# Three tiles of the MLP's up projection, instead of two, taken token group by token group

## The chip, the cores and the metric

The kernel runs on one core of one Trainium2 chip. The metric is the time of one execution in microseconds (us), the median of several runs.

## The reference, cut to what matters

Two layers of a backbone over 512 latent tokens and 256 context tokens, width 1024, in float32. Each layer ends with an MLP whose hidden width is 4096; the second layer computes it for the latent tokens alone.

```python
def sq_relu_mlp(h, w1, w2):
    return jnp.square(jax.nn.relu(h @ w1)) @ w2

        x = x + g1 * ox
        x = x + g2 * sq_relu_mlp(modulate(rmsnorm(x, norm_mlp[l]), sh2, sc2), w_ff1[l], w_ff2[l])
        if not last:
            h = h + cg1 * oc
            h = h + cg2 * sq_relu_mlp(modulate(rmsnorm(h, norm_mlp[l]), csh2, csc2), w_ff1[l], w_ff2[l])
```

## The kernel before, in words

All activations stand transposed: 128 channels on the partitions, tokens along the free axis. Latent and context tokens lie side by side, 768 columns in layer 0 and 512 in layer 1. A float32 product is made of three float32r matmuls (`mm3`, all issued by line 220): operands are split into a high part (a rounded copy, ScalarE, line 228) and a low part (the difference, VectorE, line 237), and hi x hi, hi x lo and lo x hi are summed in PSUM.

The program is a list of tasks. `emit` (line 279) walks through it; ahead of each task it starts the loads of coming weights and splits up to four pieces of 128 x 512 ahead (`AP_`), of which at most six live at once (`N_W`, tiles `wt`). The Tile scheduler then puts each engine's instructions into a fixed order; each engine runs its own in that order.

**Ahead of the MLP** the output projection's last tiles (`res`) are computed token group by token group. The groups are columns 0 to 255, 256 to 511 and, in layer 0 alone, 512 to 767. When a group's `x` is complete, its RMS norm follows: the sum of squares by a matmul (`ssum`), then per channel tile `hn` (VectorE, line 572), the high part of `h` (ScalarE, line 575) and its low part (VectorE, line 576). The norm of the last group is the list `first` in `layer_ff`.

**The MLP** (`layer_ff`, line 1347) goes by chunks of the hidden width: 4 tiles of 128 hidden channels in a chunk in layer 0, 8 in layer 1. An up tile (`up`) is 8 x 3 matmuls per part: two halves of 384 columns in layer 0, one of 512 columns in layer 1 (PSUM tiles `f`, called f1 in the order). Only the first tiles of the first chunk go another way (`up_two`, line 1455): for one token group at a time, over all k, for all of these tiles, with matmuls of 256 columns. The norm of the last group (`first`) stands in the list between group 0 and the others.

The evacuation (`evac`) takes relu (ScalarE, line 1437) and the square (line 1439) into `b`; `sums` makes the seven operands of a Strassen product from a pair of tiles and their two token halves: differences `T` (VectorE, lines 1391 and 1392), and for each operand the high part (line 228) and the low part (line 237) in `act`.

The down projection (`block`, `product`; PSUM tiles f2) multiplies them in the order A11, S1, A12, S4, S3, S2, A22 with quarters of the weights or sums of quarters (`sum`, VectorE, line 264); each product is evacuated by a gate into `x` (VectorE, line 1481), a copy to `V` (ScalarE, line 1489) or an addition to it. In layer 0 a block has two products of 6 matmuls per weight piece, in layer 1 one of 12.

Beside all this VectorE makes the adaLN modulation of later stages as dot products (`rows`, `dot`, line 492), whose weights come through three buffers.

Of the kernel before, what the change touches and what calls it, by code (L numbers as in the profile page):

```python
# [144 lines left out]
def merge(*streams):  # L145

    total = [max(sum(t.cost for t in s), 1e-9) for s in streams]
    done = [0.0] * len(streams)
    at = [0] * len(streams)
    out = []  # L150
    while True:
        live = [i for i in range(len(streams)) if at[i] < len(streams[i])]
        if not live:
            return out
        i = min(live, key=lambda j: (done[j] + 0.5 * streams[j][at[j]].cost) / total[j])
        t = streams[i][at[i]]
        at[i] += 1
        done[i] += t.cost
        out.append(t)


class Net:
# [1184 lines left out]
    def layer_ff(self, l, whole, groups, first):  # L1347
# [83 lines left out]
        def evac(c, m, half, parts):  # L1431

            if half in (0, None):
                st["b", m % 2] = self.tmp("b")
            b = st["b", m % 2]
            for ps, at, n in parts:
                nc.scalar.activation(b[:, at:at + n], ps, AF.Relu)  # L1437
            o, n = (0, w) if half is None else (half * hw, hw)
            nc.scalar.activation(b[:, o:o + n], b[:, o:o + n], AF.Square)
            if c == n_chunk - 1:  # L1440
                split_plain(c, m, half)
                return
            for i in (0, 1) if half is None else (half,):
                sums(c, m, i)

        def up(c, m, u):
            for half in (None,) if last else range(2):
                o, n = (half * hw, hw) if half is not None else (0, w)
                ps = self.B([P, 512], "f1")
                for k in range(NK):  # L1450
                    s = slice(k * P, (k + 1) * P)
                    self.mm3(ps[:, :n], u[:, 0, s], u[:, 1, s], H(k)[:, 0, o:o + n], H(k)[:, 1, o:o + n], k == 0, k == NK - 1)
                evac(c, m, half, [(ps[:, :n], o, n)])

        def up_two(us, i):

            if i == 0:
                st["pair"] = [self.R("f1") for _ in us]
            ps = st["pair"]
            o, n, _ = groups[i]  # L1460
            for k in range(NK):
                s = slice(k * P, (k + 1) * P)
                for j, u in enumerate(us):
                    self.mm3(ps[j][:, o:o + n], u[:, 0, s], u[:, 1, s],
                             H(k)[:, 0, o:o + n], H(k)[:, 1, o:o + n], k == 0, k == NK - 1)
            if i < len(groups) - 1:
                return
            for j in range(2):
                for half in range(2):
                    o, e = half * hw, half * hw + hw  # L1470
                    cut = [(max(o, x), min(e, x + 512)) for x in range(0, w, 512)]
                    evac(0, j, half, [(ps[j][:, x:y], x, y - x) for x, y in cut if x < y])
# [37 lines left out]
        def block(c, blk, u):  # L1510
            cost = 3 * CP * hw / 2.2
            return [Task(cost, lambda i=i, n=n: product(c, u, i, MP * blk + i, n), (u.pieces[n],))
                    for n in (A11, S1, A12, S4, S3, S2, A22) for i in range(MP)]

        def finish(j):

            U, v5, v7 = (st[n][j] for n in "U57")
            add(v7, v7, U)
            gate(2 * j + 1, 0, v7, True)
            add(U, U, v5)  # L1520
            add(v7, v7, v5)
            gate(2 * j, 1, U)
            gate(2 * j + 1, 1, v7, True)
# [24 lines left out]
        for c in range(n_chunk):  # L1548
            us = [Unit(a["w_ff1"][l, 2 * CP * c + m], 1024) for m in range(2 * CP)]
            m0, ups = 0, []  # L1550
            cost = self.lin_cost(NK, [(0, hw)] * 2)
            if c == 0:
                m0 = 2
                pair = [Task(2 * cost / len(groups), lambda us=us, i=i: up_two(us[:2], i), tuple(us[:2]))
                        for i in range(len(groups))]
                out += [Task(0, begin), pair[0]] + first + pair[1:]
            for m in range(m0, 2 * CP):
                ups.append(Task(cost, lambda c=c, m=m, u=us[m]: up(c, m, u), (us[m],)))
            if c == 0:
                ups.append(Task(0, negate))  # L1560
            if c == n_chunk - 1:
                ups = merge(ups, [Task(1, lambda j=j: finish(j)) for j in range(4)])
            blocks = [Unit(a["w_ff2"][l, c * n_blk + blk], 2048, "st") for blk in range(n_blk)]
            downs = []
            if c < n_chunk - 1:
                for blk in range(n_blk):
                    downs += block(c, blk, blocks[blk])
            share = -(-len(spread) // max(n_chunk - 1 - c, 1))
            extra, spread = spread[:share], spread[share:]
            if c == 0:  # L1570
                out += merge(ups, self.extra.pop(("ff1", l), []))
                out += merge(downs, extra)
            else:
                out += merge(ups, extra) + downs if l == 0 else merge(ups + downs, extra)
# [199 lines left out]
```

## Time and profile before

| | |
|---|---|
| median of 3 runs | 1567.8 us (1564.02 to 1570.93) |
| the profiled execution: its time, its span | 1565.01 us, 1562.9 us |
| TensorE (PE) busy | 1506.0 us, 96% |
| VectorE (DVE) busy | 1190.1 us, 76% |
| ScalarE (ACT) busy | 797.0 us, 51% |
| GpSimd (POOL) busy | 37.9 us, 2% |
| DMA | 191.98 MB moved, mean 123 GB/s |

Busy shares are averages over the whole span. Stretches of it have other limits, so the order of time of each engine is read at the places where the change acts: in layer 0 from about 395 to 475 us, in layer 1 from about 1195 to 1290 us. A line of the order of time gives start, length, engine, source line, operation, what is written from what, and how many instructions are merged; in square brackets stands how long the engine was idle before and what ended that.

### The profile page before, as it was taken

Reading aid. Unit: us, or ns where it says so; the run is one execution under the profiler, and the core shown is the slowest. Engines: PE = TensorE matmul, PEld = TensorE weight load, DVE = VectorE, ACT = ScalarE, POOL = GpSimd, SP = SyncE. Lnnn points to the kernel's source line nnn. Section 1 sums busy time; section 2 is a strip of 40 time slices with the busy share of each in tenths; the row PEclk is TensorE's granted clock in tenths of the full one; section 3 lists DMA queues with packets and bytes.
Section 4 is the critical chain, followed back from the end, with each engine's and each line's share of the span. In section 5 each row is a group of like instructions: output and inputs, shape, how many; then the busy total and the mean of one; then the engine's idle time right before and its main releaser. Section 6 shows DMA issues by size and latency. Waiting matters only on the chain.

```text
span 1562.9 us, 24541 instructions
## 1 busy us (share of the span) xinstructions
PE 1506.0 (96%) x9120; PEld 1329.2 (85%) x9120; DVE 1190.1 (76%) x2633; ACT 797.0 (51%) x1635; POOL 37.9 (2%) x78
## 2 busy tenths in 40 slices
PE   5999999999999999999999999989999999999997
PEld 2798667888899999999999998757888898989886
DVE  6668765887997887878869696997647895968844
ACT  4425467653654344344443463566655655455443
POOL 0110001000000000000000002001000000000000
PEclk9999999999999999999999999999999999999999
DMA  9463454555132413322223227547433443242321
GB/s 359 136 186 101 133 137 95 173 180 187 48 108 89 129 49 106 100 68 90 75 75 114 81 96 230 177 125 189 152 97 113 155 120 97 82 127 72 126 81 54
DMA packets 68903, 191.98 MB, mean 123 GB/s; under 512 B 8752, under 2 KB 11312, under 8 KB 68784
## 3 DMA queue, kind: packets, MB, share of 16 engines
q1 hardware_dynamic: 65440, 180.18, 36.6%
q0 software_dynamic: 2816, 9.70, 2.7%
q8 instruction: 72, 1.18, 0.3%
q10 hardware_dynamic: 528, 0.52, 0.1%
q14 instruction: 47, 0.39, 0.1%
HBM read 159.97 MB, written 10.49 MB: 109 GB/s over the span
## 4 chain that ended last, share of the span: by engine, by line
PE 83%; DVE 9%; ACT 3%; DMA 3%; issue 1%; SPq 0%; DVEq 0%; ACTq 0%
PE f L220 49%; PE A L220 9%; PE sc L220 4%; PE oe L220 3%; PE res L220 3%; PE pv L220 3%; PE rv L220 2%; PE pT L1052 2%; DMA rows<-w_adaT 2%; PE ada L220 1%; DVE wt L237 1%; DVE hn L572 1%; DVE h L576 1%; DVE rows L492 1%; PE ro L220 1%
## 5 line engine op out<-in xcount | busy, mean ns | idle before, releaser
L220 PE MATMUL f<-h,wt 128*128 128x384 f32 (+2 forms) x2400 | 454.3, 351 | 4.2 <-ACT h L575 3.5
L220 PEld LDWEIGHTS f<-h,wt 128*128 128x128 f32 x2400 | 416.8, 189 | 38.6 <-ACT h L575 4.5
L220 PE MATMUL f<-act,wt 128*128 128x256 f32 (+2 forms) x2664 | 410.0, 315 | 1.0 <-ACT wt L228 0.7
L220 PEld LDWEIGHTS f<-act,wt 128*128 128x128 f32 x2664 | 394.0, 188 | 15.7 <-ACT wt L228 3.5
L237 DVE TENSOR_TENSOR wt<-raw,wt 128x512 fp32r<-128x512 f32 x326 | 222.6, 687 | 101.2 <-ACT wt L228 99.9
L228 ACT ACTIVATE wt<-raw 128x512 fp32r<-128x512 f32 x326 | 198.7, 626 | 166.9 <-PE f L220 67.4
L220 PE MATMUL A<-h,wt 128*128 128x512 f32 (+1 forms) x912 | 172.9, 347 | 3.4 <-ACT h L575 2.4
L220 PEld LDWEIGHTS A<-h,wt 128*128 128x128 f32 x912 | 142.8, 190 | 29.5 <-ACT h L575 3.1
L228 ACT ACTIVATE wt<-sum 128x512 fp32r<-128x512 f32 x104 | 62.7, 629 | 126.8 <-DVE sum L264 103.4
L1437 ACT ACTIVATE b<-f 128x384 f32<-128x384 f32 (+3 forms) x100 | 50.6, 510 | 139.4 <-PE f L220 139.2
L492 DVE SCALAR_TENSOR_TENSOR rows<-rows,sbc 128x512 f32<-128x512 f32 x136 | 92.0, 685 | 8.1 <-DMA rows<-w_adaT 7.5
L220 PE MATMUL sc<-k,q 96*128 96x512 f32 (+1 forms) x384 | 87.2, 356 | 8.4 <-ACT p L1034 7.4
L220 PEld LDWEIGHTS sc<-k,q 96*128 96x128 f32 x384 | 64.4, 193 | 26.3 <-ACT p L1034 10.3
L237 DVE TENSOR_TENSOR wt<-sum,wt 128x512 fp32r<-128x512 f32 x104 | 70.3, 686 | 8.3 <-ACT wt L228 7.0
L1033 DVE TENSOR_REDUCE st<-sc 128x1 f32<-128x768 f32 x64 | 60.8, 952 | 13.7 <-PE sc L220 13.1
L1481 DVE SCALAR_TENSOR_TENSOR x<-f,mod,x 128x256 f32<-128x256 f32 (+2 forms) x148 | 69.6, 502 | 0.5 <-ACT V L1489 0.4
L1053 ACT ACTIVATE pT<-pT 128x384 f32<-128x384 f32 x128 | 56.8, 492 | 23.5 <-PE pT L1052 22.8
L228 ACT ACTIVATE act<-T 128x384 fp32r<-128x384 f32 (+1 forms) x104 | 47.3, 473 | 40.5 <-DVE T L1392 28.0
L1391 DVE TENSOR_TENSOR V<-V,f 128x384 f32<-128x384 f32 (+1 forms) x136 | 66.2, 513 | 0.1
L1034 ACT ACTIVATE p<-sc,st 128x768 f32<-128x768 f32 x64 | 57.9, 905 | 14.5 <-DVE st L1033 13.4
L220 PE MATMUL oe<-mix,wt 128*128 128x512 f32 (+1 forms) x288 | 60.8, 363 | 0.0
L237 DVE TENSOR_TENSOR act<-b,act 128x384 fp32r<-128x384 f32 (+2 forms) x94 | 47.4, 514 | 16.9 <-ACT act L228 16.9
(244 smaller groups left out, 1837.9 us busy)
## 6 DMA issues: line engine op xcount, KB each, us to landing
raw<-w_ff SPq DMA_DIRECT2D x128, 512.0 KB, 3.7
rows<-w_adaT SPq DMA_DIRECT2D x136, 256.0 KB, 3.2
raw<-w_in SPq DMA_DIRECT2D x22, 512.0 KB, 4.2
raw<-w_ada SPq DMA_DIRECT2D x16, 512.0 KB, 10.1
raw<-w_out SPq DMA_DIRECT2D x16, 512.0 KB, 4.2
rows<-w_ada SPq DMA_DIRECT2D x24, 256.0 KB, 3.1
x<-xd SPq DMA_DIRECT2D x6, 768.0 KB, 8.1
x<-xT SPq DMA_DIRECT2D x4, 768.0 KB, 6.5
```

Source lines behind the costliest of these rows:

```text
L220: return self.nc.tensor.matmul(out, l, r, start=start, stop=stop)
L228: self.nc.scalar.activation(out, src, AF.Copy, **k)
L237: return self.nc.vector.tensor_tensor(out, src, hi.bitcast(F32), op=ALU.subtract)
L492: nc.vector.scalar_tensor_tensor(out, w, 1.0, self.sbc[:, v, half], op0=ALU.mult, op1=ALU.mult, accum_out=acc[:, v, i, j:j + 1])
L572: nc.vector.scalar_tensor_tensor(t[:, :n], self.X(k)[:, o:o + n], G, self.ss[:, 1, o:o + n], op0=ALU.mult, op1=ALU.mult)
L1033: nc.vector.tensor_reduce(st[:, 0:1], ps, axis=AX, op=ALU.max, negate=True)
L1034: nc.scalar.activation(p, ps, AF.Exp, bias=st[:, 0:1], accum_out=st[:, 1:2])
L1052: nc.tensor.transpose(ps[:, kt, :], p[:, (k0 + kt) * P:(k0 + kt + 1) * P], self.ident)
L1053: nc.scalar.activation(s["pT", h, qt // 2][:, k0:k0 + 3, c], ps, AF.Copy)
L1391: add = lambda x, y, z, op=ALU.add: nc.vector.tensor_tensor(x, y, z, op=op)
L1437: nc.scalar.activation(b[:, at:at + n], ps, AF.Relu)
L1481: self.mark = nc.vector.scalar_tensor_tensor(x, ps[:, at - o:at - o + n], g[:, cond:cond + 1], x, op0=ALU.mult, op1=ALU.add)
```

## The change

The first three tiles of the first chunk are taken group by group, not two. `up` then begins with the fourth tile.

```diff
-        def up_two(us, i):
+        def up_three(us, i):
...
             if i < len(groups) - 1:
                 return
-            for j in range(2):
+            for j in range(3):
                 for half in range(2):
...
             if c == 0:
-                m0 = 2
-                pair = [Task(2 * cost / len(groups), lambda us=us, i=i: up_two(us[:2], i), tuple(us[:2]))
+                m0 = 3
+                pair = [Task(3 * cost / len(groups), lambda us=us, i=i: up_three(us[:3], i), tuple(us[:3]))
                         for i in range(len(groups))]
                 out += [Task(0, begin), pair[0]] + first + pair[1:]
```

What moves is seen in the engines' orders.

TensorE, layer 0, where group 2 begins. f1_838 and f1_839 are tiles 1 and 2 on groups 0 and 1, f1_854 and f1_855 the same tiles on group 2, and f1_873 is tile 3, columns 0 to 383. Before:

```order
L220 MATMUL f1_838_4299<-h7_790_4071,wt_770_3972 128x256 x3
L220 MATMUL f1_839_4303<-h7_790_4071,wt_820_4226 128x256 x3
L220 MATMUL f1_854_4446<-h0_783_4064,wt_769_3969 128x256
L220 MATMUL f1_855_4450<-h0_783_4064,wt_819_4223 128x256
L220 MATMUL f1_873_4555<-h0_783_4064,wt_836_4293 128x384 x3
L220 MATMUL f1_854_4446<-h0_783_4064,wt_769_3969 128x256 x2
L220 MATMUL f1_855_4450<-h0_783_4064,wt_819_4223 128x256 x2
L220 MATMUL f1_854_4446<-h1_784_4065,wt_769_3969 128x256 x3
L220 MATMUL f1_855_4450<-h1_784_4065,wt_819_4223 128x256 x3
```

Now, ahead of the same place (f1_840 is tile 3 on groups 0 and 1; group 2's f1_855 to f1_857 come after it):

```order
L220 MATMUL f1_840_4307<-h0_783_4064,wt_836_4293 128x256
L220 MATMUL f1_840_4307<-h1_784_4065,wt_836_4293 128x256 x3
L220 MATMUL f1_840_4307<-h2_785_4066,wt_836_4293 128x256 x3
L220 MATMUL f1_840_4307<-h3_786_4067,wt_836_4293 128x256 x3
L220 MATMUL f1_840_4307<-h4_787_4068,wt_837_4296 128x256 x3
L220 MATMUL f1_840_4307<-h5_788_4069,wt_837_4296 128x256 x3
L220 MATMUL f1_840_4307<-h6_789_4070,wt_837_4296 128x256 x3
L220 MATMUL f1_840_4307<-h7_790_4071,wt_837_4296 128x256 x3
L220 MATMUL f1_840_4307<-h0_783_4064,wt_836_4293 128x256 x3
L220 MATMUL f1_840_4307<-h1_784_4065,wt_836_4293 128x256 x3
```

All 48 matmuls of tile 3 on groups 0 and 1 now stand before group 2; 3 of 384 columns stood in its first rows before.

VectorE, layer 0, from the last low part of `h` to the first differences `T` of the evacuation. Before:

```order
L237 TENSOR_TENSOR wt_864_4532<-raw_771_3975,wt_864_4532 128x512
L576 SCALAR_TENSOR_TENSOR h6_789_4070<-hn_852_4390,mod0_108,h6_789_4070 128x256
L576 SCALAR_TENSOR_TENSOR h7_790_4071<-hn_853_4394,mod0_108,h7_790_4071 128x256
L237 TENSOR_TENSOR wt_865_4535<-raw_771_3975,wt_865_4535 128x512
L237 TENSOR_TENSOR act_857_4499<-b_856_4496,act_857_4499 128x384
L237 TENSOR_TENSOR wt_870_4547<-raw_821_4229,wt_870_4547 128x512
L1391 TENSOR_TENSOR T_858_4505<-b_856_4496 128x384
```

Now:

```order
L576 SCALAR_TENSOR_TENSOR h6_789_4070<-hn_853_4415,mod0_108,h6_789_4070 128x256
L576 SCALAR_TENSOR_TENSOR h7_790_4071<-hn_854_4419,mod0_108,h7_790_4071 128x256
L237 TENSOR_TENSOR act_859_4573<-b_858_4570,act_859_4573 128x384
L237 TENSOR_TENSOR wt_869_4619<-raw_771_3975,wt_869_4619 128x512
L237 TENSOR_TENSOR wt_870_4622<-raw_771_3975,wt_870_4622 128x512
L237 TENSOR_TENSOR wt_873_4629<-raw_821_4229,wt_873_4629 128x512
L1391 TENSOR_TENSOR T_860_4579<-b_858_4570 128x384
```

The same three weight pieces and one `act` stand before `T`; `T` reads `b` of tile 1, which needs group 2 of that tile.

TensorE, layer 1, where group 1 begins. Before, it follows group 0 of tiles 1 and 2 at once (f1_2258, f1_2259; f1_2289 is tile 3, 512 columns):

```order
L220 MATMUL f1_2259_12548<-h4_2230_12430,wt_2239_12467 128x256
L220 MATMUL f1_2259_12548<-h5_2231_12431,wt_2239_12467 128x256
L220 MATMUL f1_2259_12548<-h4_2230_12430,wt_2239_12467 128x256
L220 MATMUL f1_2258_12544<-h0_2226_12426,wt_2213_12334 128x256
L220 MATMUL f1_2259_12548<-h0_2226_12426,wt_2238_12464 128x256
L220 MATMUL f1_2289_12744<-h0_2226_12426,wt_2255_12536 128x512
```

Now, a little ahead of the same place (f1_2260 is tile 3):

```order
L220 MATMUL f1_2259_12573<-h4_2230_12455,wt_2239_12492 128x256
L220 MATMUL f1_2260_12577<-h0_2226_12451,wt_2255_12561 128x256 x2
L220 MATMUL f1_2260_12577<-h1_2227_12452,wt_2255_12561 128x256
L220 MATMUL f1_2260_12577<-h0_2226_12451,wt_2255_12561 128x256
L220 MATMUL f1_2260_12577<-h1_2227_12452,wt_2255_12561 128x256 x3
L220 MATMUL f1_2260_12577<-h2_2228_12453,wt_2255_12561 128x256 x3
L220 MATMUL f1_2260_12577<-h2_2228_12453,wt_2256_12564 128x256
L220 MATMUL f1_2260_12577<-h3_2229_12454,wt_2256_12564 128x256
```

The 24 matmuls of tile 3 on group 0 stand before group 1, 22 of them at this place. VectorE's order in layer 1 has, ahead of the first `T`, one weight piece (wt_2287) that stood behind it before.

## Rows read from the trace of the kernel before

**Rows 1.** The page, part 1: busy us, share of span, instructions.
```profile
PE 1506.0 (96%) x9120; PEld 1329.2 (85%) x9120; DVE 1190.1 (76%) x2633; ACT 797.0 (51%) x1635; POOL 37.9 (2%) x78
```
**Rows 2.** TensorE in order of time, layer 0, MLP start: start, us, work, [idle before].
```profile
409.70 3.71 PE L220 MATMUL f<-h,wt 128*128 128x256 f32 x28
414.93 10.36 PE L220 MATMUL f<-h,wt 128*128 128x256 f32 x72 [1.52 <-ACT h L575]
```
**Rows 3.** TensorE in order of time, layer 1, MLP start.
```profile
1203.13 2.09 PE L220 MATMUL f<-h,wt 128*128 128x256 f32 x12
1207.16 9.12 PE L220 MATMUL f<-h,wt 128*128 128x256 f32 x54 [1.95 <-ACT h L575]
```
**Rows 4.** TensorE's groups by shape: count | busy us, mean ns | idle.
```profile
L220 PE MATMUL f<-h,wt 128*128 128x384 f32 x1440 | 252.1, 337 | 0.0
...
L220 PE MATMUL f<-h,wt 128*128 128x512 f32 x720 | 170.0, 397 | 0.0
L220 PE MATMUL f<-act,wt 128*128 128x256 f32 x1296 | 157.5, 282 | 0.6 <-ACT wt L228 0.4
```
**Rows 5.** VectorE in order of time, layer 0, evacuation to the fifth weight piece.
```profile
420.12 0.89 DVE L576 SCALAR_TENSOR_TENSOR h<-hn,mod,h 128x256 fp32r<-128x256 f32 x2
...
422.02 0.56 DVE L237 TENSOR_TENSOR act<-b,act 128x384 fp32r<-128x384 f32 x1 [0.42 <-ACT act L228]
422.81 0.69 DVE L237 TENSOR_TENSOR wt<-raw,wt 128x512 fp32r<-128x512 f32 x1 [0.23 <-ACT wt L228]
423.42 0.55 DVE L1391 TENSOR_TENSOR T<-b 128x384 f32<-128x384 f32 x1
...
444.67 0.68 DVE L237 TENSOR_TENSOR wt<-sum,wt 128x512 fp32r<-128x512 f32 x1
```
**Rows 6.** ScalarE in order of time, layer 0, the same stretch.
```profile
420.91 0.52 ACT L1439 ACTIVATE b<-b 128x384 f32<-128x384 f32 x1
...
421.89 0.37 ACT L1437 ACTIVATE b<-f 128x256 f32<-128x256 f32 x1
```
**Rows 7.** Busy us by stretch, layer 0: PE, PEld, DVE, ACT, POOL, clock, DMA, GB/s.
```profile
426.00:432.00 6.00, 6.00 (x36) 6.00 (x36) 6.00 (x14) 4.58 (x11) 0.00 (x0) 1.00 0.00 0
...
462.00:468.00 6.00, 6.00 (x36) 6.00 (x35) 6.00 (x15) 4.22 (x9) 0.00 (x0) 1.00 0.65 205
...
474.00:480.00 6.00, 6.00 (x37) 6.00 (x36) 4.35 (x10) 3.00 (x6) 0.00 (x0) 1.00 0.65 208
```
**Rows 8.** TensorE in order of time, layer 0, start of the down projection.
```profile
437.61 23.79 PE L220 MATMUL f<-act,wt 128*128 128x384 f32 x132
461.67 4.60 PE L220 MATMUL f<-act,wt 128*128 128x384 f32 x25 [0.28 <-ACT wt L228]
```
**Rows 9.** VectorE in order of time, layer 1, its waits and the fifth weight piece.
```profile
1216.86 0.43 DVE L1391 TENSOR_TENSOR T<-b 128x256 f32<-128x256 f32 x1 [1.74 <-ACT b L1439]
...
1227.14 0.69 DVE L492 SCALAR_TENSOR_TENSOR rows<-rows,sbc 128x512 f32<-128x512 f32 x1 [0.45 <-DMA rows<-w_adaT]
...
1237.32 0.69 DVE L492 SCALAR_TENSOR_TENSOR rows<-rows,sbc 128x512 f32<-128x512 f32 x1 [1.54 <-DMA rows<-w_adaT]
...
1255.05 0.68 DVE L237 TENSOR_TENSOR wt<-sum,wt 128x512 fp32r<-128x512 f32 x1
```
**Rows 10.** ScalarE in order of time, layer 1, relu of tile 1 and of tile 3.
```profile
1215.56 0.66 ACT L1437 ACTIVATE b<-f 128x256 f32<-128x256 f32 x2 [1.55 <-PE f L220]
...
1220.80 0.58 ACT L1437 ACTIVATE b<-f 128x512 f32<-128x512 f32 x1
```
**Rows 11.** TensorE in order of time, layer 1, start of the down projection.
```profile
1248.46 5.79 PE L220 MATMUL f<-act,wt 128*128 128x256 f32 x48
1254.68 20.54 PE L220 MATMUL f<-act,wt 128*128 128x256 f32 x166 [0.43 <-ACT wt L228]
```
**Rows 12.** Busy us by stretch as in rows 7, around the two waits.
```profile
415.00:416.00 1.00, 1.00 (x7) 1.00 (x8) 1.00 (x4) 0.68 (x2) 0.00 (x0) 1.00 0.34 139
...
1208.00:1209.00 1.00, 1.00 (x6) 0.95 (x6) 1.00 (x4) 0.02 (x1) 0.00 (x0) 0.50 0.00 0
```

## The prediction

> **What bounds the kernel now.** I read the page's busy shares first, then TensorE's order of time where each layer's MLP begins, then VectorE's and ScalarE's behind it, and last the busy time by stretch. TensorE is busy 96% of the span [rows 1], so only a stretch in which it waits can give time back. At the start of the MLP there is one such stretch per layer. In layer 0 TensorE finishes groups 0 and 1 of the two tiles at 409.70 + 3.71 = 413.41 us and then waits 1.52 us for the first `h` of group 2 [rows 2]. In layer 1 (two groups) it is through group 0 at 1203.13 + 2.09 = 1205.22 and waits 1.95 us for `h` [rows 3]. The reader should also see that the next engine in line is VectorE. It makes `h`, and then the low halves of the weights (`wt`), the seven sums of each pair of activations (`act`, `T`) and the adaLN dot products (`rows`). In layer 0 it is busy 6.00 of 6.00 us in the slices at 426 and 462 [rows 7], and TensorE does wait there for weights, 0.28 us before 461.67 [rows 8]. Layer 1 is alike: TensorE starts the down projection at 1248.46 and waits 0.43 us for `wt` before 1254.68 [rows 11]. So the start of the MLP waits for `h`, and the start of the down projection waits for what VectorE makes.
>
> **The change, TensorE's side.** A matmul's cost is busy time by count [rows 4]: 252.1/1440 = 0.175 us at 384 columns, 170.0/720 = 0.236 at 512, 157.5/1296 = 0.1215 at 256. The third tile cost 48 of 384 in layer 0 (8.40 us) and 24 of 512 in layer 1 (5.67); as a member of the groups it costs 72 of 256 (8.75) and 48 of 256 (5.83). That adds 0.35 + 0.16 = 0.5 us, inside what follows.
>
> Layer 0: the order puts all 48 matmuls of the third tile on groups 0 and 1 ahead of group 2. 48 x 0.1215 = 5.83 us, so group 2 starts at 413.41 + 5.83 = 419.2, its `h` is then there, and the 1.52 us are gone. Group 2 is now 72 x 0.1215 = 8.75 us and ends at 428.0; the fourth tile (48 x 0.175 = 8.4) ends at 436.4. Before, the down projection began at 437.61 [rows 8]. TensorE alone would gain 1.2 us. It is not more because the old order already filled waits of group 2 with the third tile's first half.
>
> Layer 1: the old third tile (512 wide) needed both groups and could fill little. Now 24 of its matmuls stand before group 1. They fill the 1.95 us, and group 1 runs 72 x 0.1215 = 8.75 us from 1207.2 to 1216.0. The last `h` does not hold it up: only 18 of its matmuls need the last two. Before, the third tile was through at 1220.8 (its evacuation starts then [rows 10]). TensorE alone gains 4.8 us.
>
> **The change, VectorE's side.** The same activations, weights and dots are made as before, so what counts is when VectorE can begin and where it idles.
>
> Layer 0: the evacuation of tiles 1 and 2 was released by group 2. Its ScalarE relu on group 2 ran at 421.89 [rows 6], VectorE took the difference `T` at 423.42, and from the last `h` at 420.12 + 0.89 = 421.0 it had little idle [rows 5]. Now the third tile stands in between: tile 1's group 2 ends some 6 matmuls before 428.0, at 427.3, which puts the relu 5.4 us later. Behind the last `h` VectorE has in its order one `act` and three `wt`, 0.56 + 3 x 0.61 = 2.4 us of work by the same rows, and then `T`, which needs that relu (0.37) and a square (0.52) [rows 6]: 427.3 + 0.9 = 428.2 where it was 423.42, +4.8. It idles some 5 us in between. From `T` on its order is the same work, at full load, so nothing makes the delay good. The fifth weight piece of the first block (S3, from a sum) was finished at 444.67 + 0.6 = 445.3 [rows 5]; TensorE wanted it at 437.61 + 8 products of 6 x 0.175 = 446.0. Now it comes at about 450 and TensorE wants it at 436.4 + 8.4 = 444.8. It will wait some 4 us there, and at the next block's S3 (461.67 before) it will again be as late as VectorE. From 474 VectorE has slack again, 4.35 of 6 us [rows 7]. So **layer 0 loses 4.8 us**. Bounds: at least -1.2, if the delay is hidden entirely, and at most +5.9: the 5.4 of the relu and 0.5 for one gate that the new order puts ahead of that piece.
>
> Layer 1: here the evacuation does not begin later. Before, group 1's matmuls were stretched by late `h`, and the relu stood at 1215.56 [rows 10]; now tile 1's last matmul is 6 before 1216.0, at 1215.3. VectorE's `T` stays at about 1216.7 (1216.86 before [rows 9]). From there to the low half of S3, at 1255.05 + 0.6 = 1255.65 [rows 9], VectorE spent 38.8 us, of which its two waits for a `rows` transfer, 0.45 and 1.54 us [rows 9], are the idle that counts. TensorE arrives 4.8 us sooner, but S3 cannot be there sooner than VectorE: 0.2 from `T`, 0.6 from one `wt` that now falls into the idle before `T`, and 0 to 2.0 of the idle. I take 0.7 of that, because the `rows` transfers have three buffers as before and are asked for by VectorE's own progress. **Layer 1 gains 1.5 us**, bounds 0 and 4.8; TensorE then waits some 3 us between the third and fifth product.
>
> The other edits: the last group of tiles holds all six weight buffers, so the fourth tile's pieces can be made only after the middle of the last group; that is 4.4 us before TensorE wants them, against some 0.6 us per piece on each engine, so I cost it at nothing (0.6 us per layer if that cover goes). PSUM holds six banks of eight in layer 0 instead of four; VectorE's order up to group 2 is unchanged, so banks come free when they did. SP's transfers keep their order but for the place of two in layer 1.
>
> **Rule and row.** The relu at 421.89 ran while TensorE was on the third tile, up to 437.6 [rows 6, 8]: that overlap is what the change shortens. The Trainium skill, "Perfetto Trace Analysis", section Matmuls, says that independent matmul groups should rotate through PSUM banks so that the evacuation of one overlaps the matmuls of the next, and that larger matmuls are more efficient. By that rule three tiles that end together are the wrong way in both layers; the trace agrees in layer 0, and in layer 1 the late `h` had delayed the evacuation already. The sum by the rule is the second rival's.
>
> **The sum.** +4.8 - 1.5 = +3.3 us. The profiled execution took 1565.0 us, so it would become 1568.3; it lies 2.8 below the median of the runs, 1567.8, and against that I forecast **1571.1 us**, which is +0.2%: no change that can be told. 0.5% (7.8 us) is about what a measurement of this kernel can tell.
>
> **Rivals.** (1) VectorE's delay is hidden and TensorE keeps both gains: -1.2 - 4.8 = -6.0, 1561.8. For it: TensorE's idle at those places was only 0.28 and 0.43 us, so the pieces may have more room than I read. Against it: VectorE's full slices [rows 7]. (2) Slower: the evacuation comes late in layer 1 as well, because group 1 of three tiles ends later than 1215.5 by as much as in layer 0; it decides if TensorE is not yet free for group 1 at 1207.2. The price is 4.8 twice, +9.6, 1577.4. A long wait could also cost clock: after the idle before 1207.16 the granted clock was 0.50, the lower level of 1.2 GHz, at 1208, with 6 matmuls in the us; after the 1.52 us before 414.93 it stayed at 1.00 [rows 12]. The 4 us before S3 in layer 0 is longer than either. At half clock some 10 matmuls lose 0.12 to 0.18 each, 1.2 to 1.8 us, but TensorE is waiting for VectorE in that block anyway, so I add nothing. The Trainium skill, "TensorE: Matmul & The Clock Gate", Part 1, has the array fall to 1.2 GHz after idling; the rows at 1208 agree, and by that rule layer 0 would pay those 1.2 to 1.8 us on top. (3) The edit does next to nothing: the old order already mixes the third tile into group 2 in layer 0, and the losses there and the gains of layer 1 cancel, 0 +- 1, 1567.8. The order speaks against it: 48 matmuls do move ahead.
>
> **Chances.** Forecast 0.62 (+0.5 to +6), rival 1 0.13, rival 2 0.13, rival 3 0.12. The range is 1564 to 1577: the forecast's bounds plus the runs' own spread of some 3 us; it leaves out most of rivals 1 and 2. Slower by over 0.5% is most of rival 2 and a little of the forecast, 0.12; faster is a corner of rival 1, 0.04; the rest, 0.84, is within.
>
> **What would show it.** The waits of 1.52 and 1.95 us before group 2 and group 1 should be gone; the clock at 1208 should be 1.00; `T` in layer 0 some 5 us later with VectorE idle before it; a wait of TensorE for a `wt` from a sum of about 4 us before S3 in layer 0, and of 2 to 4 us in sum at the down start of layer 1. At 490 TensorE should stand about 5 us behind the old trace; layer 1 should win 4.8 of it up to the down projection and give 3 back there, so that about 3 are left at 1290. If TensorE stands ahead at 490, the delay of the evacuation was hidden and my layer 0 is wrong; if layer 1 loses time between 1190 and 1220, rival 2 holds.

## The result and the profile after

The median of 10 runs (before: the 3 of the section ahead and 7 more) rose from 1567.4 us to 1576.4 us, a ratio of 1.0055 with a 95% interval of 1.0038 to 1.0072. One run after took 2113.6 us and is left out of the ratio, as is one of 2984.4 us of l0_tilewise below. The ratio makes +8.6 us (6.0 to 11.3), just over the 0.5% that a measurement of this kernel can tell. The forecast was 1571.1, the range 1564 to 1577.

The busy times of the profile after, beside [rows 1]:

```profile
span 1575.0 us, 24643 instructions
PE 1513.5 (96%) x9168; PEld 1338.4 (85%) x9168; DVE 1189.4 (76%) x2633; ACT 796.2 (51%) x1638; POOL 38.0 (2%) x78
```

VectorE and ScalarE do the work they did. TensorE is busy 7.5 us longer, of which the added matmuls explain 0.5. The rest must be matmuls that took longer.

**Layer 0.** TensorE's order of time in the changed kernel, answering to [rows 2, 8]:

```profile
411.47 26.26 PE L220 MATMUL f<-h,wt 128*128 128x256 f32 x196
437.56 5.37 PE L220 MATMUL f<-act,wt 128*128 128x384 f32 x30
443.61 3.68 PE L220 MATMUL f<-act,wt 128*128 128x384 f32 x18 [0.68 <-ACT wt L228]
451.42 16.45 PE L220 MATMUL f<-act,wt 128*128 128x384 f32 x84 [4.12 <-ACT wt L228]
468.13 6.51 PE L220 MATMUL f<-act,wt 128*128 128x384 f32 x36 [0.28 <-ACT wt L228]
474.48 33.44 PE L220 MATMUL f<-h,wt 128*128 128x384 f32 x192
```

The wait of 1.52 us for `h` is gone and the up tiles run through. But after 48 matmuls of the down projection, ahead of S3, TensorE waits 4.12 us. VectorE's order of time shows why, beside [rows 5]:

```profile
422.81 0.56 DVE L237 TENSOR_TENSOR act<-b,act 128x384 fp32r<-128x384 f32 x1 [0.51 <-ACT act L228]
425.12 1.90 DVE L237 TENSOR_TENSOR wt<-raw,wt 128x512 fp32r<-128x512 f32 x3 [1.75 <-ACT wt L228]
429.70 0.56 DVE L1391 TENSOR_TENSOR T<-b 128x384 f32<-128x384 f32 x1 [2.69 <-ACT b L1439]
...
450.01 0.68 DVE L264 TENSOR_TENSOR sum<-raw,raw 128x512 f32<-128x512 f32 x1
...
451.97 0.68 DVE L237 TENSOR_TENSOR wt<-sum,wt 128x512 fp32r<-128x512 f32 x1
```

In the kernel before, the same `sum` stood here:

```profile
442.91 0.69 DVE L264 TENSOR_TENSOR sum<-raw,raw 128x512 f32<-128x512 f32 x1
```

VectorE idles 0.51 + 1.75 + 2.69 = 4.95 us ahead of `T`, the last and longest of it for the late `b`, and starts `T` at 429.70. The sum for S3's weight piece comes at 450.01 (before at 442.91); ScalarE takes the high half from it, which ends TensorE's wait at 451.42. The low half starts at 451.97, before at 444.67 [rows 5]. (This execution had reached the MLP 1.8 us later than the one before.) Behind the wait the clock fell, as TensorE's windows show (start and end, length, busy us, matmuls, granted clock, DMA share, GB/s):

```profile
448.00:452.00 4.00, 0.58 (x2) 0.86 0.27 78
452.00:456.00 4.00, 4.00 (x19) 0.72 0.49 184
```

4 x (0.14 + 0.28) x 2 = 3.4 us were at the lower level of 1.2 GHz. The 84 matmuls from 451.42 took 16.45 us where they take 14.75 at the pace of a later block (168 in 29.50): 1.7 us.

These 1.7 us are not part of the loss, because VectorE sets the end of this block. It is busy without a break, as in the slices of [rows 7] before, and what TensorE waits for last, until 468.13, is a weight piece that ScalarE makes as soon as VectorE's sum is there (windows with the columns of rows 7, then the sum and ScalarE's step):

```profile
450.00:456.00 6.00, 4.58 (x19) 4.43 (x20) 6.00 (x20) 3.17 (x6) 0.00 (x0) 0.72 0.51 175
456.00:462.00 6.00, 6.00 (x36) 6.00 (x35) 6.00 (x15) 1.91 (x4) 0.00 (x0) 1.00 0.47 141
462.00:468.00 6.00, 5.86 (x33) 5.21 (x31) 6.00 (x14) 2.17 (x5) 0.00 (x0) 1.00 0.11 39
...
466.67 0.68 DVE L264 TENSOR_TENSOR sum<-raw,raw 128x512 f32<-128x512 f32 x1
467.45 1.15 ACT L228 ACTIVATE wt<-sum 128x512 fp32r<-128x512 f32 x2 [2.32 <-DVE sum L264]
```

The same two steps before:

```profile
460.20 0.69 DVE L264 TENSOR_TENSOR sum<-raw,raw 128x512 f32<-128x512 f32 x1
460.98 1.15 ACT L228 ACTIVATE wt<-sum 128x512 fp32r<-128x512 f32 x2 [2.32 <-DVE sum L264]
```

From `T` to this sum VectorE takes 466.67 - 429.70 = 36.97 us, before 460.20 - 423.42 = 36.78. So `T`, 4.5 us late when the later start of 1.8 is taken off, makes the end of the wait 4.7 us late (468.13 against 461.67 [rows 8]). At full clock TensorE would have stood waiting for these pieces instead.

**Layer 1**, beside [rows 3, 11]:

```profile
1215.86 41.18 PE L220 MATMUL f<-h,wt 128*128 128x256 f32 x226
1256.88 4.03 PE L220 MATMUL f<-act,wt 128*128 128x256 f32 x33
1262.23 2.09 PE L220 MATMUL f<-act,wt 128*128 128x256 f32 x15 [1.32 <-ACT act L228]
1265.84 36.06 PE L220 MATMUL f<-act,wt 128*128 128x256 f32 x288 [1.52 <-ACT wt L228]
```

The 1.95 us are gone and group 1 runs through. At the down projection TensorE waits 1.32 + 1.52 = 2.8 us, where it waited 0.43 [rows 11]. VectorE in turn waited for a transfer, beside the two waits of [rows 9]:

```profile
1229.63 0.43 DVE L1391 TENSOR_TENSOR T<-b 128x256 f32<-128x256 f32 x1 [2.23 <-ACT b L1439]
...
1248.64 0.69 DVE L492 SCALAR_TENSOR_TENSOR rows<-rows,sbc 128x512 f32<-128x512 f32 x1 [1.80 <-DMA rows<-w_adaT]
```

**Where the 8.6 us are.** Each of the two kernels was profiled three times; the spans are 1562.9, 1566.1, 1563.8 and 1575.0, 1573.5, 1569.9, in the mean +8.5. TensorE's order of time cuts the difference into stretches (means of three, after minus before):

| stretch | us |
|---|---|
| up to 28 matmuls ahead of group 2 in layer 0 (409.70 and 411.47 in the first profiles) | +0.3 |
| A: from there to the second chunk's up projection in layer 0 | +4.7 |
| B: from there to the last chunk's | +2.8 |
| from there to layer 1's output projection of 108 matmuls | +2.1 |
| C: from there to the second chunk's up projection in layer 1 | -1.3 |
| the rest | -0.1 |

A and C are what the prediction worked out, +4.8 and -1.5. The two stretches between were not in it. In the stretch of +2.1, layer 1's attention waits longer for ScalarE's `p` (line 1034): 8.2, 8.7 and 7.8 us after, 6.3, 6.9 and 7.0 before (us in total, times, longest; the first profiles, after and before, from 840 to 1190 us):

```profile
PE sc L220 <- ACT p L1034: 8.2, 2, 4.6
PE sc L220 <- ACT p L1034: 6.3, 2, 3.3
```

### The profile page after: what moved, and what is told of

Same layout as the page of the kernel before. It is cut to its first block, busy times and chain, and to the rows that moved or that the text cites. A ratio compares the mean times of both kernels' runs of the same rounds, so it can differ in the third digit from the quotient of the medians.

```text
span 1575.0 us, 24643 instructions
## 1 busy us (share of the span) xinstructions
PE 1513.5 (96%) x9168; PEld 1338.4 (85%) x9168; DVE 1189.4 (76%) x2633; ACT 796.2 (51%) x1638; POOL 38.0 (2%) x78
## 4 chain that ended last, share of the span: by engine, by line
PE 82%; DVE 10%; ACT 4%; DMA 3%; issue 1%; SPq 0%; DVEq 0%; ACTq 0%
PE f L220 49%; PE A L220 8%; PE sc L220 4%; PE oe L220 3%; PE res L220 3%; PE pv L220 3%; PE rv L220 2%; PE pT L1052 2%; DMA rows<-w_adaT 2%; PE ada L220 1%; DVE rows L492 1%; DVE wt L237 1%; DVE act L237 1%; PE ro L220 1%; PE ssum L220 1%
## 5 line engine op out<-in xcount | busy, mean ns | idle before, releaser
L220 PE MATMUL f<-act,wt 128*128 128x256 f32 (+2 forms) x2664 | 414.2, 317 | 8.1 <-ACT wt L228 6.6
L220 PEld LDWEIGHTS f<-act,wt 128*128 128x128 f32 x2664 | 398.3, 189 | 22.7 <-ACT wt L228 9.0
L220 PE MATMUL res<-mix,wt 128*128 128x256 f32 (+1 forms) x384 | 59.6, 316 | 1.9 <-DVE om L1073 1.9
```

Source lines behind the costliest of these rows:

```text
L220: return self.nc.tensor.matmul(out, l, r, start=start, stop=stop)
```

## The experiments

Three measures run through them. A is 58.3 us before and 63.0 after; the texts on record count it from the `ssum` 14.0 us ahead, as 72.3 and 77. An asterisk marks a stretch C with a clock drop inside. B is given with the number of slow chunks, which the first experiment explains.

| kernel (profiles) | A | B | slow chunks of 7 | C |
|---|---|---|---|---|
| before (3) | 58.3, 58.3, 58.3 | 376.5, 379.1, 376.5 | 1, 3, 0 | 116.5*, 116.3*, 115.1 |
| changed (3) | 63.0, 63.0, 63.0 | 380.9, 379.9, 379.9 | 6, 4, 4 | 116.0*, 113.8, 114.2 |
| l0_three | 62.9 | 379.8 | 4 | 114.7 |
| l1_three | 58.3 | 379.1 | 3 | 113.0 |
| l0_tilewise | 59.6 | 380.8 | 5 | 115.9* |
| l0_dots_early | 58.1 | 376.5 | 0 | 115.1 |
| l1_dots_early | 58.3 | 378.9 | 4 | 112.0 |
| both_mended | 59.6 | 380.9 | 6 | 113.0 |
| both_dots_early | 58.3 | 376.4 | 0 | 114.5 |
| l0_two_dots | 57.3 | 377.2 | 2 | 116.2* |

**The two kernels again** (after_again, before_again, after_third, before_third; nothing is edited).

> The changed kernel once more, for its profile. If the slower pitch belongs to its instruction order, the 192 up matmuls of a chunk in layer 0 take 34.08 us again from the second chunk on; if it is set anew in each execution, some or all chunks take 33.44 us. The waits at the two MLP starts repeat within 0.5 us by either.

> The kernel before once more, for its profile. If the pitch belongs to the instruction order, 192 up matmuls take 33.44 us in chunks two to seven and 34.08 in the last, as in its first profile; if it is set anew in each execution, chunks of 34.08 us turn up elsewhere. The clock drops at 40, 1064, 1105 and 1218 us repeat if they follow from waits of the program.

> The changed kernel a third time, for its profile: 4 or more of 7 up chunks at 34.08 us if the slow pitch goes with it, 0 to 3 if it is chance; layer 0 up to its second chunk 76.8 to 78.6 us, layer 1's stretch 113 to 116, the longer values with a clock drop inside.

> The kernel before a third time, for its profile: 1 to 4 of 7 up chunks at 34.08 us if its pitch is as in the profiles that share its layer 0; layer 0's stretch 72.3 us, layer 1's 114.7 to 116.5.

Measured: 1575.6 and 1568.2 us, then 1572.1 and 1565.8. In before_again, TensorE's order of time from the middle of layer 0's MLP reads:

```profile
468.12 33.44 PE L220 MATMUL f<-h,wt 128*128 128x384 f32 x192
501.40 29.57 PE L220 MATMUL f<-act,wt 128*128 128x384 f32 x168
530.81 34.08 PE L220 MATMUL f<-h,wt 128*128 128x384 f32 x192
564.73 29.84 PE L220 MATMUL f<-act,wt 128*128 128x384 f32 x168
...
721.64 33.44 PE L220 MATMUL f<-h,wt 128*128 128x384 f32 x192
```

The same 192 matmuls take 33.44 or 34.08 us, with no wait and at full clock: 174.2 or 177.5 ns each. A slow chunk costs 0.64 us here and some 0.35 in its down projection. TensorE goes from one pace to the other within an execution, at other chunks in each one: the kernel before had 1, 3 and 0 slow chunks of 7 though nothing was edited. So a pace is no fixed property of the instruction order. Yet the changed kernel had 6, 4 and 4, as expected of "goes with it". before_third, expected to have 1 to 4, had none.

The clock drops differ as well. (The text on record counts from some 11 us earlier: its 1218 is the drop of [rows 12] at 1208.) Windows of 24 us in layer 1's attention have granted clocks of 0.93, 0.86 and 0.93 in before_third from 1024, 1048 and 1096 us. The same program before had 1.00, 0.86 and 0.96 there, with 0.97 from 1072.

**One layer at a time** (l0_three, l1_three). The number of tiles became a pair, one per layer:

```diff
-                m0 = 3
+                m0 = (3, 2)[l]      # l1_three: (2, 3)[l]
```

> Three tiles by groups in layer 0 only; layer 1 is as in the kernel before. My sum: +4.8 us (a wait of 4 to 5 us for the wt from a sum before the product S3 of the first block), so 1572 us beside 1567.4. Rival, the whole +9 us of the change comes from layer 0: the wait, a clock drop behind it of up to 1.7 us, and the slower pitch of the 384-column matmuls that follows (176.7 ns in place of 173.3, +4.4 us by 889 us): +9 to +11 us, 1577 us, with the pitch at 176.7 ns again in the profile.

> Three tiles by groups in layer 1 only; layer 0 is as in the kernel before. My sum: layer 1 alone is worth -1.5 us (TensorE 4.2 to 4.8 us ahead at its down projection, some 3 given back there in waits for act and wt), so 1566 us beside 1567.4. Rival, layer 1 costs time as well: +3 to +5 us. On the pitch of the 384-column matmuls in layer 0 (173.3 ns before, 176.7 ns from 530 us on in the changed kernel): if the edit of layer 0 sets it, it stays at 173.3 ns here until 840 us, as before; if it is set anew in each execution, it may differ with the same layer 0.

Measured: layer 0 alone 1574.0 beside 1569.0 us, ratio 1.0034 (1.0017 to 1.0052), +5.3; layer 1 alone 1569.7, ratio 1.0003 (0.9988 to 1.0018), +0.5 (-1.9 to +2.8). Layer 0's loss stands without layer 1's edit: A is 62.9, with the same wait of 4.12 us. The rival of +9 from layer 0 alone is outside its interval. Layer 1 alone is neither confirmed nor excluded by the times, but C, 113.0, is shorter than in any profile with two tiles there. TensorE's order of time in l1_three:

```profile
1207.84 41.17 PE L220 MATMUL f<-h,wt 128*128 128x256 f32 x226
1248.86 5.79 PE L220 MATMUL f<-act,wt 128*128 128x256 f32 x48
1256.12 34.78 PE L220 MATMUL f<-act,wt 128*128 128x256 f32 x288 [1.48 <-ACT wt L228]
1290.74 45.13 PE L220 MATMUL f<-h,wt 128*128 128x512 f32 x192
```

Here VectorE waited for no `rows` transfer, and the wait for `act` is gone. The changed kernel's profiles, with 0.87, 1.04 and 1.80 us of that wait, have C of 113.8, 114.2 and 116.0 (the last with 1 us or more from its clock drop). Within 0.2 us C is 113.0 plus this wait of VectorE, so in these four profiles that part of the idle time counts in full.

**Layer 0: evacuate each tile as it ends** (l0_tilewise).

```diff
+            whole_tile = l in (0,) and i == len(groups) - 1
+            steps = [(k, j) for j in range(len(us)) for k in range(NK)] if whole_tile else [(k, j) for k in range(NK) for j in range(len(us))]
+            for k, j in steps:
...
+                if whole_tile and k == NK - 1:
+                    out_tile(j, ps[j])
```

(`out_tile` calls `evac` on the two halves of one tile.)

> Three tiles in layer 0 only, and in the last token group the matmuls run tile by tile, each tile evacuated as it ends. My theory (the loss is the late evacuation): tile 1 ends 5.8 us sooner, T comes at about 424.5 us from the same start in place of 429.7, the wait of 4.1 us before S3 shrinks to 0 to 1.5, and layer 0 up to its second chunk takes 72 to 73.5 us in place of 77 (72.3 before). Rival (the third tile's weights and PSUM buffers delay S3): wait and 77 us stay.

VectorE's and TensorE's order of time:

```profile
425.23 0.55 DVE L1391 TENSOR_TENSOR T<-b 128x384 f32<-128x384 f32 x1
```

```profile
437.51 8.48 PE L220 MATMUL f<-act,wt 128*128 128x384 f32 x48
447.49 8.85 PE L220 MATMUL f<-act,wt 128*128 128x384 f32 x48 [1.49 <-ACT wt L228]
457.43 6.92 PE L220 MATMUL f<-act,wt 128*128 128x384 f32 x36 [1.10 <-ACT wt L228]
464.63 6.52 PE L220 MATMUL f<-act,wt 128*128 128x384 f32 x36 [0.28 <-ACT wt L228]
```

`T` comes 4.5 us sooner than in the change, the wait of 4.12 becomes 1.49, and the clock drop is gone; a wait of 1.10 us comes later in the block. A is 59.6 us, +1.3 where the change has +4.7; counted as in the text on record, 73.6, a little above its upper end. So the late evacuation is what most of the 4.7 us come from; a quarter stays. It lies behind `T`, which is back in its place (13.8 us after the row at 411.41; before 13.7): the edit reorders VectorE's work as well, and what part of that costs the 1.3 us was not tried. The time is 1572.4 beside 1567.9, ratio 1.0024 (1.0006 to 1.0043): +3.8, more than A gives, with 5 slow chunks.

**Layer 0: take VectorE's dot products out of the way** (l0_dots_early). Three tiles, evacuated late, but the four tasks of `ff1` (eight dot products) are listed before the last group:

```diff
+                dots = self.extra.pop(("ff1", l), [])
+                early, self.extra["ff1", l] = dots[:(4, 0)[l]], dots[(4, 0)[l]:]
-                out += [Task(0, begin), pair[0]] + first + pair[1:]
+                out += [Task(0, begin), pair[0]] + first + pair[1:-1] + early + pair[-1:]
```

> Three tiles in layer 0 only, its evacuation late as in the change, but the eight adaLN dot products (0.61 us each) that stood between T and S3 on VectorE are put into its idle time before T. My theory (VectorE's work from T on sets S3): 4.4 to 4.9 us leave that stretch, so the wait of 4.1 us before S3 falls to 0 to 0.7 and layer 0 takes 72.5 to 73.5 us in place of 77. Rival (ScalarE's or the weights' own chain sets S3): the wait stays at 3 to 4 us.

VectorE's `T` and TensorE's down projection:

```profile
427.71 0.55 DVE L1391 TENSOR_TENSOR T<-b 128x384 f32<-128x384 f32 x1
```

```profile
435.49 8.84 PE L220 MATMUL f<-act,wt 128*128 128x384 f32 x48
445.49 15.57 PE L220 MATMUL f<-act,wt 128*128 128x384 f32 x84 [1.16 <-ACT V L1489]
461.34 6.51 PE L220 MATMUL f<-act,wt 128*128 128x384 f32 x36 [0.28 <-ACT wt L228]
467.68 12.64 PE L220 MATMUL f<-h,wt 128*128 128x384 f32 x72
```

`T` comes as late as in the change (18.15 us after the row at 409.56; there 18.23), now without idle time before it, and the wait of 4.12 us for S3's weight piece is gone. What is late next is ScalarE's copy to `V`, 1.16 us. A is 58.1, 0.2 less than before. The time is 1567.8 beside 1567.9, ratio 1.0004 (0.9991 to 1.0017), and no chunk is slow. VectorE's work from `T` on was the limit: the whole loss of layer 0 goes when 4.9 us of it go, with the evacuation as late as ever.

**The control: dot products early with two tiles** (l0_two_dots; `m0` is 2, the edit above otherwise).

> Two tiles in both layers, as before; only layer 0's eight dot products are put early, as a control. My theory: they are worth something only where VectorE idles before T; here it doesn't, T comes 4 us later and the work behind it is 4.9 us less, so layer 0 takes 72.3 us, plus or minus 0.5, and the time is unchanged, 1568. Rival (the early dots gain by themselves): 71 us or less in layer 0.

A is 57.3: 1.0 less than before, between what the theory and its rival said. VectorE was not quite hidden in the kernel before either: the wait of 0.28 us at 461.67 [rows 8] is gone, and the 168 matmuls of the block run through in 29.56 us. The time does not show it: 1565.8 beside 1564.9, ratio 1.0004 (0.9992 to 1.0016). So of the early dots' 4.9 us in A (63.0 to 58.1), 1.0 is to be had without the third tile, and with early dots on both sides the third tile still costs 0.8 us (57.3 to 58.1).

**Layer 1: dot products early** (l1_dots_early; `m0` is (2, 3) and the pair of the diff above is (0, 3)).

> Three tiles in layer 1 only, with three of its 16 dot products (1.8 us) put into VectorE's idle 2.2 us before T. My theory (VectorE's work sets the start of the down projection there): the waits of 0.5 to 1.3 and 1.5 us fall to under 1 us in sum, the stretch from the output projection to the second chunk falls from about 113 to 111.5 us. Rival (the rows transfers or the activations set it): it stays at 113.

TensorE's order of time:

```profile
1208.78 41.18 PE L220 MATMUL f<-h,wt 128*128 128x256 f32 x226
1249.80 5.86 PE L220 MATMUL f<-act,wt 128*128 128x256 f32 x48
1256.24 34.62 PE L220 MATMUL f<-act,wt 128*128 128x256 f32 x288 [0.58 <-ACT wt L228]
```

VectorE's idle time before `T` falls from 2.23 us to 0.40, TensorE's wait from 1.48 to 0.58 and C from 113.0 to 112.0, with 0.52 us lost to a `rows` transfer. The time is 1565.7 beside 1567.9, ratio 0.9988 (0.9974 to 1.0002). It is the lowest ratio of the study, better than the change (1.0055), but not told apart from the kernel before.

**Both layers mended** (both_mended: tile by tile in layer 0, three dots early in layer 1; both_dots_early: eight and three dots early).

> Three tiles in both layers, layer 0 tile by tile in the last group, layer 1 with three dot products early. By my theory layer 0 costs 0 to +1 us and layer 1 gives 2.5 to 3.5: 1565 to 1567 us beside 1568. If the loss of the change lies elsewhere (clock or pitch that follow from the third tile itself), it stays at 1573 to 1576.

> Three tiles in both layers with the dot products early in both (eight in layer 0, three in layer 1). By the stretches measured so far layer 0 takes 72.1 us (72.3 before) and layer 1 112 to 112.5 us (115 before), so -3 us: 1565 us beside 1568. If layer 0's late evacuation costs something later, or the slower pitch comes with three tiles, 1568 or more. The pitch in layer 0 tells too: 0 of 7 chunks slow with this layer 0 so far, 4 to 6 of 7 in the other kernels that have three tiles there, 1 to 4 with two.

Measured: 1570.3 beside 1567.9, ratio 1.0015 (0.9998 to 1.0032), and 1566.6 beside 1564.9, ratio 1.0013 (1.0004 to 1.0023). Both take back most of the change's loss, and neither reaches the gain expected. In the first, A (+1.3) is a little above what was expected, C (113.0) gives 2.1 us against the kernel before without a clock drop (115.1) and 3.4 with one, and 6 of 7 chunks were slow. In the second, A is 58.3 and no chunk is slow, but C is 114.5 in place of 112 to 112.5. VectorE's order of time in both_dots_early:

```profile
1237.59 0.69 DVE L492 SCALAR_TENSOR_TENSOR rows<-rows,sbc 128x512 f32<-128x512 f32 x1 [2.68 <-DMA rows<-w_adaT]
```

VectorE waited 2.68 us for a transfer for which l1_dots_early, with the same layer 1, waited 0.52: the difference is 2.2 us, and C's is 2.5. What makes the transfer late in one and not in the other was not tried.

## Why the prediction was right, and where it fell short

- **Layer 0's sum, +4.8: measured +4.7, and by its mechanism.** `T` came 4.5 us late where 4.8 were worked out, VectorE made none of it good, and at the next block's S3 TensorE was again as late as VectorE, as the prediction has it. TensorE's own sums were less exact: alone it gained 1.8 us up to the down projection (409.70 to 437.61 before, 411.47 to 437.56 after), not 1.2, and its waits there grew by 4.12 + 0.68 = 4.8. The clock drop came, and the 1.2 to 1.8 us priced for it hold the 1.7 measured. The step "TensorE is waiting for VectorE in that block anyway, so I add nothing" held: VectorE had no idle time from the drop to the last piece, and A is its delay. This is read from the trace; no execution had the wait without the drop. In l0_three the room was just enough: no wait follows the drop there, and A is 62.9. The Trainium skill, "TensorE: Matmul & The Clock Gate", Part 1, has the array fall to 1.2 GHz after idling; the windows at 448 and 452 us agree. The sum by that rule put the cost on top of the +4.8; the runs have it under VectorE's delay.
- **The reason, VectorE's work behind a late `T`: shown**, from both sides. An earlier evacuation (l0_tilewise) took 3.4 of the 4.7 us away, and less work behind a late one (l0_dots_early) all of it, 1.0 of that being had without the third tile. The Trainium skill, "Perfetto Trace Analysis", section Matmuls, wants the evacuation of one group of matmuls under the next; in l0_tilewise, which does that, A fell from 63.0 to 59.6.
- **Layer 1's sum, -1.5: measured -1.3 in the three pairs of profiles.** TensorE came to its down projection 4.3 us sooner ([rows 11] against 1256.88, with the 12.7 us by which this execution was already late at the MLP's start), for 4.8 forecast, and gave 3.8 back (in the mean of three pairs 3.9 and 2.6). Of the 4.3, 1.3 are the clock drop that the kernel before has at 1208 [rows 12] and the change has not: in l0_three, with the old layer 1 and no drop, the up tiles from the same row take 40.12 us, not 41.46. So part of the agreement is luck: without a clock drop on either side C is 115.1 before and 114.0 after, -1.0. Of the 2.0 us of `rows` waits I took 0.7 off, which leaves 1.3; the runs show 1.80, 0.87 and 1.04 with the change.
- **Rival 1** (VectorE's delay hidden) and **rival 3** (nothing happens) fall with the 4.12 us wait. **Rival 2** has the time, but not its mechanism: its +9.6 needed the evacuation late in layer 1 as well, and layer 1 gained. Its clock drop was real, but hidden.
- **The signs** came: both `h` waits gone, `T` 6.3 us later (4.5 after the later start), a wait of 4 us before S3 and of 2.8 at layer 1's down start, TensorE 4.7 us behind at the second chunk of layer 0 (6.5 with the later start), and no clock drop at layer 1's first tiles (before_third had none either). The sign for 1290 us, three behind, did not: TensorE was 6.5 to 12.2 us behind at the second chunk in the three pairs.
- **What the sum lacked.** The forecast lies 5.3 us under the median, and +8.6 is outside the +0.5 to +6 that it gave itself. The range holds 1576.4 by 0.6 us, through the 3 us of spread put around those bounds, and "slower by over 0.5%", which 1.0055 just reaches, had a chance of 0.12. A and C together are +3.4, for +3.3 in the sum; that the whole still fell within the range is luck. The sum ended each layer at its second chunk and took the work behind as unmoved. The profiles put +2.8 us there in the rest of layer 0's MLP, in slow chunks, and +2.1 from its last chunk to layer 1's output projection, where the waits for `p` are 1.5 us longer in the mean and some of it may be clock drops (windows with 0.93, 0.93, 0.86, 0.86 in after_again, where before_again has 0.93, 0.86, 0.93). I priced matmuls at one mean duration each [rows 4], which hides that there are two.

**What stays open.** Whether the change brings the slower pace with it. The six profiles with three tiles and a late or tile-wise evacuation in layer 0 have 4 to 6 slow chunks (B of 379.8 to 380.9), the six with two tiles 0 to 4 (376.5 to 379.1), the two with three tiles and early dots none. That fits a cause in layer 0's order, and fits chance less well, but it is one to three executions per kernel, and nothing in the profile says why TensorE takes one pace or the other. The waits for `p` are open in the same way: 6.9 to 8.7 us in the eight profiles with three tiles in layer 0, 5.2 to 7.0 in the six with two. So of the +8.5 us between the profiles, 4.9 have no cause shown. Layer 1's `rows` wait is open too.

## What to carry to other kernels

Taking more tiles through a stage together fills the wait at its start, but lets all their evacuations begin at its end; where the evacuating engine has no slack in the next stage, its delay comes back as a wait there. A clock drop behind such a wait adds nothing as long as that engine still sets when the stage ends, so follow its order of time, and not only TensorE's, before adding the drop to a sum. The idle time that this leaves on that engine can be filled: moving independent work into it was worth more (4.9 us of A, or 3.9 beyond what it gives without the change) than evacuating earlier (3.4). When a change is worth a few us of 1570, compare it by stretches in repeated profiles, since the rest of the program alone moved by as much.

## What was not expected of the hardware

- TensorE ran the same 192 matmuls of 384 columns, without waits and at full clock, in 33.44 or in 34.08 us, changing pace within one execution; over a layer's MLP this alone moved stretch B by up to 4.5 us (376.4 to 380.9).
- A wait of 4.12 us was followed by 3.4 us at the lower clock in all four profiles with that wait (the 84 matmuls behind it took 1.7 us longer in the first); the waits of 1.49 us in l0_tilewise and both_mended were not followed by one. A wait of 1.9 us ahead of layer 0's MLP was followed by a drop in some executions of one program and not in others (before_third, but not before or before_again).
